# RWKV trunk: one substitution for the triangular inverses of two batches

## The chip, the cores and the metric

One core of a Trainium2 chip runs one program. TensorE (PE) multiplies, VectorE (DVE), ScalarE (ACT) and GpSimd (POOL) work element by element, SyncE (SP) issues most DMAs. The metric is the device time of one execution in microseconds. The shapes are one sequence of 512 tokens with 1024 features, all in float32.

## The reference

The model has two layers. Layer 0 mixes tokens with RWKV-7, layer 1 with a spatial gating unit; each is followed by a SwiGLU feed-forward network, and each of the four parts has a norm ahead of it and one behind it. The change touches the RWKV-7 mixer alone. Its core is a recurrence over the 512 tokens for each of 16 heads of 64 features:

```python
def step(S, inp):
    r_t, w_t, k_t, v_t, a_t, b_t = inp
    sa = jnp.einsum('bhij,bhj->bhi', S, a_t)
    S = (S * w_t[:, :, None, :]
         + sa[..., None] * b_t[:, :, None, :]
         + v_t[..., None] * k_t[:, :, None, :])
    y = jnp.einsum('bhij,bhj->bhi', S, r_t)
    return S, y
```

k, r and v are projections of differently mixed inputs; w (the decay) and a come from small two-layer projections; after the recurrence come a group norm per head, a bonus term, a gate and the output projection.

## The kernel before, in words

The kernel does the recurrence by chunks of 64 tokens, 8 chunks per head. Inside a chunk the terms with a and b form a lower triangular matrix of 64 x 64 whose inverse (of identity minus it) is needed once per head and chunk. The 1024 features are taken in four batches b of 256 features, which is 4 heads, so 32 matrices of 64 x 64 a batch. A matrix is cut in four blocks of 32: the two on the diagonal are inverted, and the block below is put together from them by products.

The work is written in stages, each for one batch: P (projections of k and r), E (`early`: decay, its cumulated sums, the scaled copies that go to the scratch tensors sa and sb in HBM), F (`front`), B (`back`), S (`scan`, the state from chunk to chunk), N (group norm, gate). X makes the mixed input for v, split in a high and a low part for three-pass products, and V multiplies it with the weights of v for one batch. X holds eight tiles `xsp` of 128 features; the string XV says in which pool of SBUF each of them lives: x (the pool of the input tiles), s and e (pools whose slots other tiles of the same size use too).

`front` loads ST and MV from scratch, multiplies them (`lm`, L709: four products for four chunks of one head), and takes three things from each result: VectorE masks a part into MV (L712), ScalarE copies the triangular part to LA (L715) and another part to BX (L716). `bkt` (L722) are transposes by products, copied by ScalarE to BX (L726, L727).

`back` inverts. VectorE transposes LA in blocks of 32 to LX (L735). POOL multiplies LA by a mask (L738), so that only the blocks of 16 below the diagonal of each block of 32 stay for the later products. Then a substitution of 15 steps runs on VectorE, with two instructions each (L744 product, L746 sum into Dm), on all 128 diagonal blocks of 16 of the batch at once (m16 is the mask's column). Dm starts as identity, which POOL writes in `front` (L696, L697). Two block transposes give Dn (L749, in the tile `hn`) and Dt (L750). From there TensorE joins blocks: Qp (L766, from LA and Dn), Qs on VectorE, Np and Tp (L775, L778), copies to Dn2 and bdT, Q2p (L789), a copy, T2p (L798), a copy to bdT (L802). `mvt` (L757) transposes MV; mp (L807) multiplies MVt with the finished inverse, ScalarE copies the result (L809), and gh (L814) multiplies on; VectorE adds the results into MV (L816, L817). `scan` takes MV (us L843, Yp L856).

What sets the order: the list PLAN gives the order in which the stages are recorded. A scheduler of the framework, which simulates the recorded program, then sets the order on each engine from the recorded order, the dependences and its own idea of times. Slots of SBUF are given out in the recorded order too: a tile waits until the last reader of the slot's former tile is done. Each engine runs its own queue strictly in order. `E3` is the last early stage; its chain ends on VectorE with `ta` (L662) and on POOL with two products (L669 with r, L670 with kp), after which `bps` (L665, the bonus term) and the stores to sb follow.

Of the kernel before, what the change touches and what calls it, by code (L numbers as in the profile page):

```python
# [32 lines left out]
PLAN = "P0 E0 P1 P2 E1 P3 E2 E3 X0 F0 B0 F1 V0 V1 V2 V3 B1 S0 F2 S1 F3 N0 B2 N1 B3 S2 N2 S3 N3".split()  # L33
XV = "xxxessss"
# [48 lines left out]
class Trunk:  # L83
# [287 lines left out]
    def rwkv(self, x0, nxt):  # L371
# [3 lines left out]
        with ExitStack() as ctx:  # L375
# [23 lines left out]
            def gslot(name, shape):  # L399
                return self.gp.tile(shape, F32, name=name, tag="gain", bufs=2)  # L400
# [21 lines left out]
            m16 = mk2[:, 0, 0:C:16]  # L422
# [184 lines left out]
            diag = lambda t: t[:, :, 0:512].rearrange("p b (t s) -> p b t s", s=32)  # L607

# [69 lines left out]
            def front(b, o):  # L678
# [13 lines left out]
                LA = e2("LA", (P, 2, NC, C))  # L692
                Dm = self.f0p.tile([P, 2, 528], F32, name="Dm", tag="f0", bufs=2)
                for hd in range(2):
                    g.memset(LA[64 * hd + 32:64 * hd + 64, :, :, 0:32], 0.0)
                g.memset(full(Dm), 0.0)  # L696
                g.memset(Dm.rearrange("p b r -> p (b r)")[:, 0:1024:33], 1.0)  # L697
                for hh, q in units:
# [6 lines left out]
                    for hd in range(2):  # L705
                        rows, other = head[hd], head[1 - hd]
                        lm = self.bank("pl", "lm")
                        for cc in range(4):
                            mm(lm[:, cc * P:(cc + 1) * P], st[:, cc].rearrange("p n t -> p (n t)"), mv[:, :, cc, hd, :], start=True, stop=True)  # L709
                        lv = lm.rearrange("p (c a t) -> p c a t", c=4, a=2)  # L710
                        la = LA[:, q, 4 * hh:4 * hh + 4]
                        v.tensor_tensor(mv[other, :, :, hd].rearrange("p a c t -> p c a t"), lv[other],  # L712
                                        mk2[other].unsqueeze(1).broadcast_to([64, 4, 2, C]), op=ALU.mult)
                        for z, x in ((64 * hd, 0), (64 * hd + 32, 32)):
                            a.copy(la[z:z + 32, :, x:C], lv[z:z + 32, :, 0, x:C])  # L715
                        a.copy(bx[rows, 1], lv[rows, :, 1, :])  # L716
# [11 lines left out]
                o.update(MV=MV, BX=BX, LA=LA, Dm=Dm)  # L728

            def back(b, o):  # L730

                MV, BX, LA, Dm = (o[n] for n in ("MV", "BX", "LA", "Dm"))
                LX = e2("LX", (P, 2, 528))

                v.transpose(full(LX), LA.rearrange("p q c (x t) -> p t (q c x)", x=2))  # L735
                LAu = LA.rearrange("p q c t -> p (q c) t")
                LAs = LA.rearrange("p q c (x t) -> p (q c) x t", t=16)
                g.tensor_tensor(LAs, LAs, m16.unsqueeze(1).unsqueeze(3).broadcast_to([P, 16, 4, 16]), op=ALU.mult)  # L738
# [8 lines left out]
                Dt = rp.tile([P, 16, 2, 32], F32, name="Dt", tag="hid", bufs=1)  # L747
                Dn = self.sm.tile([P, 16, 2, 32], F32, name="hn", tag="hn", bufs=2)
                v.transpose(Dn.rearrange("p u x s -> p s (u x)"), full(Dm).rearrange("p t s -> p s t"))  # L749
                v.transpose(Dt.rearrange("p u x t -> p t (u x)"), full(Dm))  # L750
# [13 lines left out]
                for u in range(16):  # L764
                    for z, hd, x in quarters:
                        mm(Qp[z:z + 32, u * 32:(u + 1) * 32], LAu[z:z + 32, u, 32 * x:32 * x + 32], Dn[z:z + 32, u, x, :],  # L766
                           start=True, stop=True)
# [4 lines left out]
                for u in range(16):  # L772
                    for z, hd, x in quarters:
                        if x == 0:
                            mm(Np[z:z + 32, u * 32:(u + 1) * 32], Dt[z:z + 32, u, x, :], Qs[z:z + 32, u, :], start=True, stop=True)  # L775
                for u in range(16):
                    for z, hd, x in quarters:
                        mm(Tp[z:z + 32, u * 32:(u + 1) * 32], Qs[z:z + 32, u, :], Dt[z:z + 32, u, x, :], start=True, stop=True)  # L778
# [8 lines left out]
                for u in range(16):  # L787
                    for z in (0, 64):
                        mm(Q2p[z + 32:z + 64, u * 32:(u + 1) * 32], LAu[z:z + 32, u, 32:64], Dn2[z:z + 32, u, :],  # L789
                           start=True, stop=True)  # L790
# [159 lines left out]
            for n in PLAN:  # L950
# [188 lines left out]
```

## Time and profile before

| | |
|---|---|
| median of 3 runs | 1424.42 us (1421.11 to 1426.13) |
| the profiled execution | 1426.41 us, span 1424.7 us |
| busy TensorE, VectorE, ScalarE, POOL | 1338.3, 791.8, 569.1, 274.5 us |
| share of TensorE in the chain that ended last | 77% (VectorE 7%) |

A row of the grouped view gives the line, the engine, the operation, output and inputs by the program's names, the count, then busy time in us and mean ns of one, then the idle time of the engine ahead of them and what ended it. A row of a time line gives start and length in us; the bracket behind it is idle time of that engine and what released it. A row of the waits reads: who <- for whom: us in total, times, longest. The table of stretches has for each engine busy time and count of instructions, then the granted clock of TensorE as a share of the full one, the share of busy DMA and GB/s. The profile counts most products twice: where the order has 4 `lm`, the trace has 8.

### The profile page before, as it was taken

How to read it: one execution, taken by the hardware profiler on the slowest of the kernel's cores; microseconds unless marked ns; L12 is line 12 of the kernel's file. 1: busy time of each engine (PE TensorE's matmuls, PEld its weight loads, DVE VectorE, ACT ScalarE, POOL GpSimd, SP SyncE). 2: the span in 40 equal slices, each digit the busy share in tenths (PEclk: the TensorE clock that was granted, in tenths of full speed). 3: DMA queues.
4: the chain of work that ended last, by engine and by line, in shares of the span. 5: the costliest groups of instructions: out<-in, count | busy, mean ns of one | idle time of the engine just before them, and what ended most of it. 6: DMA issues, size and time to landing. Idle time of an engine off the chain costs nothing.

```text
span 1424.7 us, 21481 instructions
## 1 busy us (share of the span) xinstructions
PE 1338.3 (94%) x8472; PEld 1091.2 (77%) x8472; DVE 791.8 (56%) x1318; ACT 569.1 (40%) x1060; POOL 274.5 (19%) x248
## 2 busy tenths in 40 slices
PE   5899997987889979999999999999999999999998
PEld 3576686976768768888888888778888888888886
DVE  6962776388685775554544222865575455443223
ACT  5654665363723363323322122743363232322221
POOL 6154463133311231111111000210121111110000
PEclk9999998987969989999999999999999999999999
DMA  5133467351322423333332232343213333332331
GB/s 157 30 107 92 127 182 200 94 150 43 87 65 88 130 90 104 89 89 103 90 99 94 89 118 74 104 129 109 89 52 112 103 89 89 103 90 103 89 96 67
DMA packets 210324, 143.04 MB, mean 100 GB/s; under 512 B 59664, under 2 KB 185136, under 8 KB 210224
## 3 DMA queue, kind: packets, MB, share of 16 engines
q1 hardware_dynamic: 208544, 135.90, 32.2%
q0 software_dynamic: 1680, 5.77, 1.3%
q8 instruction: 67, 1.10, 0.3%
q14 instruction: 33, 0.27, 0.1%
HBM read 125.39 MB, written 14.16 MB: 98 GB/s over the span
## 4 chain that ended last, share of the span: by engine, by line
PE 77%; DVE 7%; ACT 2%; issue 2%; DMA 2%; POOL 1%; SPq 1%; DVEq 0%; POOLq 0%; ACTq 0%
PE gu L158 12%; PE gu L156 12%; PE gu L157 12%; PE acc L156 8%; PE acc L157 8%; PE acc L158 8%; PE gh L814 2%; PE lm L709 2%; PE u L156 1%; PE u L158 1%; PE u L157 1%; PE Yp L856 1%; PE mp L807 1%; PE proj L158 1%; PE proj L156 1%
## 5 line engine op out<-in xcount | busy, mean ns | idle before, releaser
L131 ACT CAST whi<-wraw 128x1024 fp32r<-128x1024 f32 x161 | 168.8, 1050 | 472.5 <-PE gu L157 257.2
L132 DVE TENSOR_TENSOR wlo<-wraw,whi 128x1024 fp32r<-128x1024 f32 x161 | 246.6, 1532 | 197.2 <-ACT whi L131 193.2
L157 PE MATMUL gu<-hT,whi 128*128 128x512 f32 (+1 forms) x768 | 289.6, 378 | 4.4 <-DVE hT L59 4.4
L156 PE MATMUL gu<-hT,whi 128*128 128x512 f32 (+1 forms) x768 | 290.2, 380 | 0.8 <-ACT hT L57 0.8
L158 PE MATMUL gu<-hT,wlo 128*128 128x512 f32 (+1 forms) x768 | 289.7, 378 | 0.0
L157 PEld LDWEIGHTS gu<-hT,whi 128*128 128x128 f32 x768 | 146.0, 190 | 34.0 <-DVE hT L59 4.7
L156 PEld LDWEIGHTS gu<-hT,whi 128*128 128x128 f32 x768 | 145.8, 191 | 29.5 <-ACT hT L57 1.0
L158 PEld LDWEIGHTS gu<-hT,wlo 128*128 128x128 f32 x768 | 145.8, 190 | 29.0 <-issue 0.2
L157 PE MATMUL acc<-wlo,act 128*128 128x512 f32 x416 | 163.9, 394 | 0.0
L156 PE MATMUL acc<-whi,act 128*128 128x512 f32 x416 | 163.6, 394 | 0.0
L158 PE MATMUL acc<-whi,act 128*128 128x512 f32 x416 | 160.5, 394 | 0.0
L333 POOL TENSOR_TENSOR sg<-sg,hn 128x512 f32<-128x512 f32 x44 | 56.7, 1288 | 422.5 <-DVE sg L332 422.5
L332 DVE TENSOR_TENSOR sg<-sg,gu 128x512 f32<-128x512 f32 x44 | 30.2, 687 | 142.5 <-PE gu L158 141.1
L148 POOL TENSOR_TENSOR wlo<-wraw,whi 128x1024 fp32r<-128x1024 f32 x28 | 70.1, 2505 | 169.9 <-ACT whi L147 151.1
L158 PEld LDWEIGHTS acc<-whi,act 128*128 128x128 f32 x416 | 78.2, 188 | 18.1
L156 PEld LDWEIGHTS acc<-whi,act 128*128 128x128 f32 x416 | 78.2, 188 | 18.0
L157 PEld LDWEIGHTS acc<-wlo,act 128*128 128x128 f32 x416 | 78.1, 188 | 18.0
L330 DVE TENSOR_TENSOR sg<-gu,hn 128x512 f32<-128x512 f32 x44 | 30.4, 691 | 67.8 <-PE gu L158 67.6
L131 ACT CAST act<-sg 128x512 fp32r<-128x512 f32 x52 | 32.3, 622 | 72.2 <-POOL sg L333 58.1
L158 PE MATMUL proj<-xsp,wlo 128*128 128x512 f32 x128 | 53.7, 421 | 0.0
L156 PE MATMUL proj<-xsp,whi 128*128 128x512 f32 x128 | 51.9, 405 | 0.4 <-ACT k L529 0.4
L709 PE MATMUL lm<-MV,ST 128*128 128x128 f32 x256 | 41.6, 316 | 11.2 <-DMA ST<-sb 7.9
(305 smaller groups left out, 2248.8 us busy)
## 6 DMA issues: line engine op xcount, KB each, us to landing
wraw<-in_ffn_w_gate_dram SPq DMA_DIRECT2D x44, 512.0 KB, 3.6
wraw<-in_ffn_w_up_dram SPq DMA_DIRECT2D x44, 512.0 KB
wraw<-in_ffn_w_down_dram SPq DMA_DIRECT2D x44, 512.0 KB, 3.6
wraw<-in_rwkv_w_rkv_dram SPq DMA_DIRECT2D x24, 512.0 KB, 3.5
wraw<-in_sgu_w_in_dram SPq DMA_DIRECT2D x16, 512.0 KB, 3.6
x<-in_x_dram SPq DMA_DIRECT2D x8, 512.0 KB, 3.7
MV<-sa SPq DMA_DIRECT2D x64, 64.0 KB, 2.6
ST<-sb SPq DMA_DIRECT2D x8, 512.0 KB, 4.5
```

Source lines behind the costliest of these rows:

```text
L131: self.nc.scalar.copy(hi, src)
L132: self.nc.vector.tensor_tensor(lo, src, hi.bitcast(F32), op=ALU.subtract)
L148: nc.gpsimd.tensor_tensor(lo, raw, hi.bitcast(F32), op=ALU.subtract)
L156: mm(out, lhs[0], rhs[0], start=start, stop=False)
L157: mm(out, lhs[0], rhs[1], start=False, stop=False)
L158: mm(out, lhs[1], rhs[0], start=False, stop=stop)
L330: nc.vector.tensor_tensor(sg, pp[0], yb, op=ALU.mult)
L332: nc.vector.tensor_tensor(sg, sg, pp[1], op=ALU.mult)
L333: nc.gpsimd.tensor_tensor(sg, sg, yb, op=ALU.mult)
L709: mm(lm[:, cc * P:(cc + 1) * P], st[:, cc].rearrange("p n t -> p (n t)"), mv[:, :, cc, hd, :], start=True, stop=True)
L807: mm(mp[:, cc * P:(cc + 1) * P], bdT[:, q * NC + 4 * hh + cc].rearrange("p h t -> p (h t)"), mt[:, cc, :], start=True, stop=True)
L814: mm(gh[:, cc * P:(cc + 1) * P], mt[rows, cc, :], bx[rows, 0:2, cc, :], start=True, stop=True)
```

## The change

Batches 0 and 1, and batches 2 and 3, share one substitution. There is a new stage I (`inverses`, n = 0 or 1), recorded after the fronts of both batches. LA is now a tile of (P, 2, 2, 8, 32) for both batches with the diagonal blocks of 32 alone, a second tile LB of the same size holds the blocks below the diagonal, and one transpose, one substitution and two transposes back do for all 256 diagonal blocks of 16 of a pair. Before, half of LX and Dm held blocks off the diagonal, whose result no product read. `front` fills LA and LB with three copies of 32 x 128 for each head's `lm` (L719, L720, L721) where there were two copies, one of them of double width; the memset of LA's empty blocks is gone, and Dm is written once for a pair. POOL's mask product is replaced by a ScalarE activation with a scale per partition (f16, L744) and a memset on POOL (L745). Dn moves from the pool of `hn` to the e slots.

PLAN is changed too: V0 to V3 stand after F0 and ahead of F1, and I0, B0, B1 follow F1; I1 stands after F3. XV becomes "xxxxeegs": tiles 4 and 5 of the input for v live in e slots, tile 6 in a slot of the pool "gain", which holds two tiles and in E3 is that of the cumulated sums, tile 7 in s.

```diff
-PLAN = "P0 E0 P1 P2 E1 P3 E2 E3 X0 F0 B0 F1 V0 V1 V2 V3 B1 S0 F2 S1 F3 N0 B2 N1 B3 S2 N2 S3 N3".split()
-XV = "xxxessss"
+PLAN = "P0 E0 P1 P2 E1 P3 E2 E3 X0 F0 V0 V1 V2 V3 F1 I0 B0 B1 S0 F2 S1 F3 I1 N0 B2 N1 B3 S2 N2 S3 N3".split()
+XV = "xxxxeegs"
...
-            m16 = mk2[:, 0, 0:C:16]
+            f16 = rp.tile([P, 1], F32, name="f16")
+            for r in range(0, P, 32):
+                a.copy(f16[r:r + 32], mk2[r:r + 32, 0, (16 if r % 64 == 0 else 48):][:, 0:1])
...
-                    new = dict(x=xslot, s=s4, e=e2)[where[kt]]
+                    new = dict(x=xslot, s=s4, e=e2, g=gslot)[where[kt]]
...
-                LA = e2("LA", (P, 2, NC, C))
-                Dm = self.f0p.tile([P, 2, 528], F32, name="Dm", tag="f0", bufs=2)
-                for hd in range(2):
-                    g.memset(LA[64 * hd + 32:64 * hd + 64, :, :, 0:32], 0.0)
-                g.memset(full(Dm), 0.0)
-                g.memset(Dm.rearrange("p b r -> p (b r)")[:, 0:1024:33], 1.0)
+                if b % 2 == 0:
+                    LA, LB = (e2(n, (P, 2, 2, NC, 32)) for n in ("LA", "LB"))
+                    Dm = self.f0p.tile([P, 2, 528], F32, name="Dm", tag="f0", bufs=2)
+                    g.memset(full(Dm), 0.0)
+                    g.memset(Dm.rearrange("p b r -> p (b r)")[:, 0:1024:33], 1.0)
+                    lower[b // 2] = LA, LB, Dm
+                LA, LB, _ = lower[b // 2]
...
-                        for z, x in ((64 * hd, 0), (64 * hd + 32, 32)):
-                            a.copy(la[z:z + 32, :, x:C], lv[z:z + 32, :, 0, x:C])
+                        z = 64 * hd
+                        a.copy(la[z:z + 32], lv[z:z + 32, :, 0, 0:32])
+                        a.copy(lb[z:z + 32], lv[z:z + 32, :, 0, 32:64])
+                        a.copy(la[z + 32:z + 64], lv[z + 32:z + 64, :, 0, 32:64])
...
+            def inverses(n):
+                LA, LB, Dm = lower.pop(n)
                 LX = e2("LX", (P, 2, 528))
-                v.transpose(full(LX), LA.rearrange("p q c (x t) -> p t (q c x)", x=2))
-                LAu = LA.rearrange("p q c t -> p (q c) t")
-                LAs = LA.rearrange("p q c (x t) -> p (q c) x t", t=16)
-                g.tensor_tensor(LAs, LAs, m16.unsqueeze(1).unsqueeze(3).broadcast_to([P, 16, 4, 16]), op=ALU.mult)
+                LAu, LBu = (t.rearrange("p b q c t -> p (b q c) t") for t in (LA, LB))
+                v.transpose(full(LX), LAu.rearrange("p u t -> p t u"))
+                a.activation(LAu[:, :, 16:32], LAu[:, :, 16:32], AF.Copy, scale=f16[:, 0:1])
+                g.memset(LAu[:, :, 0:16], 0.0)
...
-                Dn = self.sm.tile([P, 16, 2, 32], F32, name="hn", tag="hn", bufs=2)
+                Dn = e2("Dn", (P, 32, 32))
...
+                return LAu, LBu, Dn, Dt
+
+            def back(b, o, inv):
+                MV, BX = o["MV"], o["BX"]
+                LAu, LBu, Dn, Dt = (t[:, b % 2 * 16:b % 2 * 16 + 16] for t in inv)
...
+                elif f == "I":
+                    inv = inverses(b)
                 elif f == "B":
-                    back(b, ops[b])
+                    back(b, ops[b], inv)
```

Line numbers move: in the changed kernel L709 is L713, L722 is L728, L735 is L742, L744 and L746 are L751 and L753, L749 and L750 are L756 and L757, L757 is L770, L766 is L779, L802 is L814, L807 is L819, L814 is L826; in `early`, L669 and L670 are L672 and L673.

The scheduler makes the order on the engines from this. Three places follow. First TensorE just after the two `ssp` (sums of squares) of E3; the number behind a name is that of the tile. Before:

```order
L709 MATMUL lm_1526<-MV_1478,ST_1476 128x128 x4
L647 MATMUL ssp_1389<-tw_1349,bones_135 128x512
L156 MATMUL v_2317<-whi_2321,xsp_1431 128x256
L157 MATMUL v_2317<-wlo_2322,xsp_1431 128x256
L158 MATMUL v_2317<-whi_2321,xsp_1431 128x256
```

The change:

```order
L650 MATMUL ssp_1390<-tw_1354,bones_135 128x512
L650 MATMUL ssp_1394<-tw_1354,bones_135 128x512
L713 MATMUL lm_1521<-MV_1483,ST_1481 128x128 x4
L713 MATMUL lm_1531<-MV_1483,ST_1481 128x128 x4
L668 MATMUL bps_1404<-hsel_141,ta_1355 64x2 x16
L728 MATMUL bkt_1542<-ident_79,ST_1481 128x128 x4
L713 MATMUL lm_1554<-MV_1490,ST_1481 128x128 x4
L156 MATMUL v_1650<-whi_1708,xsp_1472 128x256
L157 MATMUL v_1650<-wlo_1709,xsp_1472 128x256
```

Before, products of v with tiles that were ready followed at once, and `bps` stood far behind; now `bps` and the first `bkt` are ahead of them, and the next product of v reads xsp_1472, which is tile 6. On ScalarE its cast stands here in the change:

```order
L653 ACTIVATE tw_1354<-tw_1354 128x1024
L719 COPY LA_1513<-lm_1521 32x128
L719 COPY LA_1513<-lm_1531 32x128
L720 COPY LB_1514<-lm_1521 32x128
L721 COPY LA_1513<-lm_1521 32x128
L722 COPY BX_1518<-lm_1521 64x256
L720 COPY LB_1514<-lm_1531 32x128
L721 COPY LA_1513<-lm_1531 32x128
L722 COPY BX_1518<-lm_1531 64x256
L131 CAST xsp_1472<-xs_1469 128x512
```

Before, all tiles of the input for v were cast ahead of the L653's equivalent; now one is cast after the first copies of the front. LA_1513 takes the slot of E3's r, LB_1514 that of E3's k, and xsp_1472 that of E3's cumulated sums. The second place is TensorE ahead of the first Qp. Before:

```order
L156 MATMUL v<-whi,xsp 128x256
L157 MATMUL v<-wlo,xsp 128x256
L158 MATMUL v<-whi,xsp 128x256
L766 MATMUL Qp<-hn,LA 32x32 x64
```

The change:

```order
L713 MATMUL lm<-MV,ST 128x128 x12
L728 MATMUL bkt<-ident,ST 128x128 x4
L713 MATMUL lm<-MV,ST 128x128 x4
L728 MATMUL bkt<-ident,ST 128x128 x4
L770 MATMUL mvt<-ident,MV 128x128 x24
L779 MATMUL Qp<-Dn,LA 32x32 x64
L787 MATMUL Np<-Qs,Dt 32x32 x32
L790 MATMUL Tp<-Dt,Qs 32x32 x64
```

Between the last `lm` of F1 and the first Qp there are now 4 `bkt` and 24 `mvt`, and no product of v is left behind it; before, products of v stood on both sides of each of these groups. The third place is TensorE ahead of the third Qp, that of batch 2, in the change:

```order
L713 MATMUL lm<-MV,ST 128x128 x4
L868 MATMUL Yp<-su,MV 64x64 x3
L728 MATMUL bkt<-ident,ST 128x128 x4
L770 MATMUL mvt<-ident,MV 128x128 x24
L939 MATMUL yt<-ident,Y 128x128 x4
L779 MATMUL Qp<-Dn,LA 32x32 x64
L156 MATMUL gate<-sg,g2h 128x512
```

Before, the third Qp came in pieces between the `lm` of F3 (24, 3, 1, 11, 10, 3, 6 and 6 of 64); now it stands behind the last of them.

More of the change, by code (lines that the diff above doesn't have):

```diff
@@ L397, in xslot, with gslot @@
                 return self.xp.tile(shape, dt, name=name, tag="x", bufs=TT)
-            def gslot(name, shape):
-                return self.gp.tile(shape, F32, name=name, tag="gain", bufs=2)
+            def gslot(name, shape, dt=F32):
+                return self.gp.tile(shape, dt, name=name, tag="gain", bufs=2)
             mk2 = rp.tile([P, 2, C], F32, name="mk2")
@@ L607, in rwkv @@
             diag = lambda t: t[:, :, 0:512].rearrange("p b (t s) -> p b t s", s=32)
+            lower = {}
             def early(b, k, r):
@@ L746, in back @@
                     v.tensor_tensor(Dmd[:, :, j + 1:16, 0:j + 1], Dmd[:, :, j + 1:16, 0:j + 1], tv, op=ALU.add)
-                Dt = rp.tile([P, 16, 2, 32], F32, name="Dt", tag="hid", bufs=1)
-                Dn = self.sm.tile([P, 16, 2, 32], F32, name="hn", tag="hn", bufs=2)
-                v.transpose(Dn.rearrange("p u x s -> p s (u x)"), full(Dm).rearrange("p t s -> p s t"))
-                v.transpose(Dt.rearrange("p u x t -> p t (u x)"), full(Dm))
+                Dt = rp.tile([P, 32, 32], F32, name="Dt", tag="hid", bufs=1)
+                Dn = e2("Dn", (P, 32, 32))
+                v.transpose(Dn.rearrange("p u s -> p s u"), full(Dm).rearrange("p t s -> p s t"))
+                v.transpose(Dt.rearrange("p u t -> p t u"), full(Dm))
+                return LAu, LBu, Dn, Dt
+            def back(b, o, inv):
+                MV, BX = o["MV"], o["BX"]
+                LAu, LBu, Dn, Dt = (t[:, b % 2 * 16:b % 2 * 16 + 16] for t in inv)
                 MVt = {}
@@ L765, in back @@
                     for z, hd, x in quarters:
[L766 to L767 removed]
+                        mm(Qp[z:z + 32, u * 32:(u + 1) * 32], LAu[z:z + 32, u, :], Dn[z:z + 32, u, :], start=True, stop=True)
                 Qs = el("Qs", (P, 16, 32))
@@ L788, in back @@
                     for z in (0, 64):
-                        mm(Q2p[z + 32:z + 64, u * 32:(u + 1) * 32], LAu[z:z + 32, u, 32:64], Dn2[z:z + 32, u, :],
+                        mm(Q2p[z + 32:z + 64, u * 32:(u + 1) * 32], LBu[z:z + 32, u, :], Dn2[z:z + 32, u, :],
                            start=True, stop=True)
```

10 lines of the change are left out of this document (4 added, 6 removed).

## The prediction

> **What bounds the kernel now.** I read the page's busy table first, then the stretches of 25 us with the granted clock, then TensorE's waits, then the time lines around the inverses.
>
> ```profile
> PE 1338.3 (94%) x8472; PEld 1091.2 (77%) x8472; DVE 791.8 (56%) x1318; ACT 569.1 (40%) x1060; POOL 274.5 (19%) x248
> ```
> ```profile
> core 0: us, PE busy (x) PEld busy (x) DVE busy (x) ACT busy (x) POOL busy (x), PEclk, DMA share, GB/s
> 188.00:425.00 237.00, 197.13 (x2696) 174.16 (x2698) 163.69 (x315) 118.86 (x286) 76.34 (x89) 0.85 0.41 114
> 550.00:880.00 330.00, 330.00 (x1421) 266.73 (x1420) 137.92 (x133) 91.06 (x110) 30.66 (x24) 1.00 0.32 97
> ```
> 94% would say that TensorE's work is all that counts, and after 550 us it is: not a gap in 330 us, clock 1.00. The change lies in 188 to 425 us, and there TensorE stands for 237.0 - 197.1 = 39.9 us and has a mean clock of 0.85. This stage is a chain across engines; what is to be read is what TensorE waits for, and what covers each wait.
>
> ```profile
> PE mp L807 <- DVE bdT L802: 12.5, 2, 7.3
> PE lm L709 <- DMA ST<-sb: 7.9, 2, 4.6
> PE Qp L766 <- issue: 4.0, 1, 4.0
> ```
> ```profile
> 391.60:396.90 5.30, 0.00 (x0) 0.00 (x0) 5.27 (x14) 0.00 (x0) 1.80 (x1) 0.50 0.14 51
> 396.90:415.50 18.60, 17.22 (x78) 14.54 (x78) 17.95 (x40) 5.45 (x10) 3.46 (x3) 0.50 0.21 71
> 415.50:418.00 2.50, 2.50 (x19) 1.99 (x18) 0.57 (x2) 0.34 (x1) 0.00 (x0) 1.00 0.15 52
> ```
> The largest wait is for T2p's copies (L802), and VectorE is full beside it (5.27 of 5.30 us): the substitution of the next batch stands in its queue. After it TensorE works for 18.6 us at half clock, 17.2 of them busy. These waits are what the change can give back.
>
> **What is removed.** The substitution is fixed work per instruction, so two of four vanish:
>
> ```profile
> L744 DVE TENSOR_TENSOR tm<-LX,Dm 128x30 f32<-128x30 f32 (+7 forms) x60 | 22.3, 372 | 1.2
> L746 DVE TENSOR_TENSOR Dm<-Dm,tm 128x30 f32<-128x30 f32 (+7 forms) x60 | 21.0, 350 | 1.3
> L749 DVE STREAM_TRANSPOSE hn<-Dm 128x1024 f32<-128x1024 f32 x4 | 8.5, 2126 | 0.1
> L750 DVE STREAM_TRANSPOSE Dt<-Dm 128x1024 f32<-128x1024 f32 x4 | 7.9, 1976 | 0.0
> L735 DVE STREAM_TRANSPOSE LX<-LA 128x1024 f32<-128x1024 f32 x4 | 7.8, 1952 | 0.8 <-ACT LA L715 0.8
> L738 POOL TENSOR_TENSOR LA<-LA,mk 128x1024 f32<-128x1024 f32 x4 | 10.8, 2712 | 3.3 <-DVE nr_y L174 2.0 <-DVE mu L878 1.2
> L715 ACT COPY LA<-lm 32x256 f32<-32x256 f32 x32 | 11.6, 361 | 29.6 <-DVE MV L712 29.2
> L715 ACT COPY LA<-lm 32x128 f32<-32x128 f32 x32 | 8.2, 257 | 0.4
> ```
> VectorE loses half of 22.3 + 21.0 + 8.5 + 7.9 + 7.8 = 67.5, that is 33.7 us. POOL loses L738, 10.8 us, and half the memsets of Dm. ScalarE gets 96 copies of the shorter form (0.257, 24.7 us) for 11.6 + 8.2 = 19.8: +5 us over four fronts, and two mask operations of about 0.5. Nobody waits for these sums as such. B1 and B3 now find their inverse ready; I give the change the whole 12.5 us at L802 for that, and take the price of the new places next.
>
> **V0 meets the end of E3.** The order shows it: after the two `ssp` TensorE has 12 `lm`, `bps` and 4 `bkt`, then products on xsp_1472. That is tile 6 of XV, which now sits in a "gain" slot that was E3's `cum`. Its cast stands on ScalarE behind eight copies into LA, LB and BX; those of LA take the slot of E3's `r`, those of LB that of E3's `k`. So it waits for POOL's L669 and L670. In the trace before these end late, and it costs nothing, as v covers it:
>
> ```profile
> 198.74 1.41 DVE L712 TENSOR_TENSOR MV<-lm,mk 64x512 f32<-64x512 f32 x2
> 200.07 2.25 DVE L132 TENSOR_TENSOR wlo<-wraw,whi 128x1024 fp32r<-128x1024 f32 x1
> 206.49 1.42 DVE L653 SCALAR_TENSOR_TENSOR k<-k,nkk,tw 128x512 f32<-128x512 f32 x2 [3.57 <-ACT tw L650]
> 212.92 1.95 DVE L662 SCALAR_TENSOR_TENSOR ta<-r,vecT,kp 128x512 f32<-128x512 f32 x2
> 215.27 2.19 POOL L669 TENSOR_TENSOR r<-r,Pp 128x1024 f32<-128x1024 f32 x1
> 217.41 2.36 POOL L670 TENSOR_TENSOR kp<-kp,cum 128x1024 f32<-128x1024 f32 x1
> ```
> ```profile
> 195.52 0.68 PE L709 MATMUL lm<-MV,ST 128*128 128x128 f32 x4 [3.23 <-DMA ST<-sb]
> 199.22 0.28 PE L157 MATMUL v<-wlo,xsp 128*128 128x256 f32 x1
> 199.34 0.28 PE L158 MATMUL v<-whi,xsp 128*128 128x256 f32 x1
> ```
> Products of v come every 0.12 us there, about 118 of them (14 us) between 199 and 220. In the new order neither the split of wlo (2.25 us, ahead of the second `tw`) nor the L712 of the later `lm` (three, 0.7 each) stand between E3's operations, and `tw` waits less for ScalarE; I let `ta` end at 209.5, not 214.9; L669 ends at 211.9 (2.19), L670 at 214.2 (2.36), the cast at about 215. TensorE can do 12 `lm`, `bps` and `bkt`, about 3 us, between 199 and 215.5: **13 us more idle**. Bounds: nothing, if E3 ran so far ahead that the cast is done by 202; and 19 us, if L670 ends at 219.8 as now. I stand nearer the upper end, since the chain from `k` to L670 alone is 206.49 to 219.77 = 13.3 us and cannot begin before ssp.
>
> **I0 has no cover.** The batches' order was B0 after F0, with V and F1 to fill. Now LX needs F1's last `lm`, and the order has all of V before it; between the last `lm` and Qp stand only 4 `bkt` and 24 `mvt`. From 215.5 the work is 312 products of v at 0.12 = 37.4, and by the rows
>
> ```profile
> 213.34 1.05 PE L709 MATMUL lm<-MV,ST 128*128 128x128 f32 x8
> 202.57 0.60 PE L722 MATMUL bkt<-ident,ST 128*128 128x128 f32 x4
> ```
> (the profile counts an `lm` twice, so 4 of the order are 8 here) 52 `lm` 14 and 28 `bkt` 4.2, and I add 7 for gates, weights and another wait for ST like the one of 4.6: last `lm` at 278. Then the copies to LA and LB (1), LX 1.95, thirty operations, and Dn:
>
> ```profile
> L744 DVE TENSOR_TENSOR tm<-LX,Dm x60: 173/270/2345, 224.8 to 408.4; 128x30 f32<-128x30 f32 x8, 128x56 f32<-128x56 f32 x8, 128x78 f32<-128x78 f32 x8, 128x96 f32<-128x96 f32 x8
> 245.34 2.21 DVE L749 STREAM_TRANSPOSE hn<-Dm 128x1024 f32<-128x1024 f32 x1
> 334.00 2.35 DVE L744 TENSOR_TENSOR tm<-LX,Dm 128x110 f32<-128x110 f32 x1
> 333.87 2.34 POOL L900 TENSOR_TENSOR Y<-Y,gn 128x1024 f32<-128x1024 f32 x1 [3.65 <-DVE Y L885]
> ```
> An operation takes 0.27 us in the median (the second number of the first row), thirty with small gaps 9 us; the 20 us from the first at 224.8 to Dn at 245.34 hold much else. Qp0 starts at 278 + 1 + 2 + 9 + 2.2 = 292, not 249.4; `mvt` (at the price of `bkt`, 24 x 0.15) takes 3.6 us of it, so **11 us are idle**. Bounds: 8 (if copies and gaps cost nothing) and 22 (as long as batch 0 takes now).
>
> **B0, B1, S0, F2, S1, F3.** Before, 132 products of v (16 us) lay between Qp0 and Qp1; now none, and B0's chain (Qp, Qs, Np and Tp, a copy, Q2p, a copy, T2p, a copy, then mp and gh) stands bare, some 5 us of it idle.
>
> ```profile
> 249.36 1.29 PE L766 MATMUL Qp<-hn,LA 32*32 32x32 f32 x128
> 265.42 0.83 PE L807 MATMUL mp<-MVt,bdT 128*128 128x128 f32 x6
> 293.75 1.71 PE L814 MATMUL gh<-BX,MVt 64*128 64x128 f32 x16
> ```
> Qp to mp was 16.1 us with 61 products of v between (7.3): bare 9. mp to the end of the last gh was 30.0 us with 71 of them (8.5) and 12 `lm` of F1: bare 20. Qp1 stands at 321. From there to F3's last `lm` TensorE has 64 `lm` (17), 32 `bkt` (5), 32 gh and 16 mp (11), the scans (9), B1's chain (5), gates and waits: 56 us, to 378.
>
> **I1 has no cover either**, and N1's group norm stands between its operations. In the order Qp2 is behind 24 `mvt` and 4 `yt`. Of the pure 15 us (LX to Dn, as at I0), the norm's five wide operations and small ones add 6.4 (about 1.2 us each, as L885 below); beside POOL's norm a VectorE operation took 2.35 us in place of 0.27, and two such add 4: 25.5 us, Qp2 at 404. **About 19 us are idle.** The chain's bounds are 15 (no norm, no POOL) and 32, what batch 3 took (from LX at 380.2 to Dn's end):
>
> ```profile
> 380.16 1.95 DVE L735 STREAM_TRANSPOSE LX<-LA 128x1024 f32<-128x1024 f32 x1
> 398.44 1.22 DVE L885 TENSOR_TENSOR Y<-Y,nr_y 128x1024 f32<-128x1024 f32 x1
> 410.55 2.06 DVE L749 STREAM_TRANSPOSE hn<-Dm 128x1024 f32<-128x1024 f32 x1
> 424.86 0.77 PE L766 MATMUL Qp<-hn,LA 32*32 32x32 f32 x67
> ```
> Then Qs is behind Dt, `ob` and a split of weights, mp2 at 417; mp2 to Qp3 took from 396.9, where TensorE's wait of 5.30 ends, to 424.86 = 28 us before, 18 of them at half clock, which doubled some 9 us of work. I take 23: **Qp3 at 440**, not 424.9. From Qp3 on both orders are alike.
>
> **Sum.** The profiled execution took 1426.41 us (span 1424.7), 2 us above the runs' median of 1424.42. 440 - 425 = +15: **1441 us**. A ledger beside it: +13 + 11 + 19 of new idle time and 5 at B0, 48; less 12.5 at L802, 4.6 at F1's ST (V0 to V3 are ahead of it now), 4 at Qp and 9 of half clock, 30: +18. I keep the walk's 15.
>
> Half clock is the term I am least sure of. The rows show it from 391.6 to 415.5 although TensorE was hardly idle from 396.9 on. The Trainium skill, TensorE: Matmul & The Clock Gate, Part 1 (The HAM clock gate), has the array at half rate after one idle window of about 3.4 us, and back after about 3.4 us of sustained work; the 18 us here contradict the second half. By that rule each of three new stretches costs 1.7 us of lag, 5 in all, and the sum would be 1446. By the row it is up to 9 each; the 23 us above hold 4 of it for one stretch.
>
> **The rivals.**
> *Faster, 1413 (0.20).* VectorE's queue is the mechanism. If E3's chain, freed of 5 us of VectorE work, ends so early that the cast is there by 205 (3 us idle, not 13), and I1 takes 18 us as L738 and half the substitution are gone, Qp3 is 440 - 10 - 7.5 = 422; with the half clock of 391 to 415 gone too (9), 413: 12 us saved. For it: 163.7 us of VectorE in the stage become 130, and 76.3 of POOL some 64. Against: the waits at xsp_1472 and LX are of dependence, not load. It decides from 20 us less than my three idle terms of 43 and the half clock.
> *No change, about 1426 (0.14).* The three idle terms at two thirds (29 of 43 us) take 14 off the walk: Qp3 at 426.
> *Worse, 1459 (0.16).* The walk has no half clock after the new idle stretches at E3 and I0; with 9 us after each, as after 396.9, Qp3 is at 458. For it: those 18 us at 0.50 follow a gap shorter than either. Against: between 550 and 880the clock is whole throughout, and I cannot see in the trace what ends a slow stretch.
>
> **How the numbers follow.** My forecast of 1441, with its own range of 1430 to 1450, has 0.50. A measurement of this kernel tells some 0.3%, 4 us, from no change. Below 1420 lies the faster rival (0.20), within 4 us of 1424 the second with an edge of my own case (0.14), the rest is slower: 0.66. The range has to leave out no more than 0.2: from 1418, which takes a part of the faster case, to 1460, the worse case's middle.
>
> **What would show it.** Right: TensorE idle before the first product on xsp_1472, its cast released by POOL's L673; idle of some 10 us ahead of the first Qp and over 15 ahead of the third, both put down to the transposes into Dn; no wait at T2p's copies; VectorE near 758 us busy. Wrong: no gap at 200 to 215, or Qp2's wait under 10 us, or TensorE's idle time in the stage below 40 us. If F2 and F3 run longer than 60 us between Qp1 and LX, ScalarE's copies set the pace, and the worse case holds for another reason than clock.

## The result and the profile after

| | before | after |
|---|---|---|
| median of the runs | 1424.03 us (1421.11 to 1426.13, 4 runs) | 1468.8 us (1455.06 to 1478.82, 4 runs) |
| ratio | 1 | 1.0281, 95% interval 1.0226 to 1.0335 |
| profiled execution | 1426.41 us, span 1424.7 | 1468.59 us, span 1466.9 |
| mean granted clock | 0.962 | 0.937 |

The changed kernel is slower by 45 us by the medians and by 40 by the ratio; 1441 had been predicted. One of its four runs, 1478.82, was in a slower state and is not in the ratio; the other three took 1455.06, 1468.59 and 1469.01 us. So every difference to this kernel is uncertain by some 8 us, and the profiled execution is not its fastest. The busy table of the page after:

```profile
PE 1351.8 (92%) x8472; PEld 1102.8 (75%) x8472; DVE 761.7 (52%) x1252; ACT 573.3 (39%) x1098; POOL 255.5 (17%) x234
```

VectorE did lose 30.1 us (791.8 to 761.7) and POOL 19. But the span grew by 42.2 us, of which 13.5 are TensorE's own busy time (1351.8 - 1338.3) with the same 8472 products, and the other 28.7 are idle time. Stretches show where: up to the fourth Qp; B0's chain and its dense part; the wait at I1; from the third group of mp, and from the fourth Qp, to the first product of the feed-forward network (`gu`). After:

```profile
core 0: us, PE busy (x) PEld busy (x) DVE busy (x) ACT busy (x) POOL busy (x), PEclk, DMA share, GB/s
188.00:452.90 264.90, 199.67 (x2688) 178.00 (x2688) 133.01 (x252) 122.90 (x324) 52.86 (x69) 0.79 0.35 98
285.60:327.10 41.50, 36.12 (x616) 32.20 (x616) 11.70 (x25) 9.42 (x21) 3.11 (x6) 0.54 0.09 21
302.00:323.70 21.70, 21.20 (x113) 18.30 (x113) 5.01 (x14) 4.03 (x10) 3.11 (x6) 0.50 0.13 29
390.40:413.20 22.80, 5.98 (x28) 4.29 (x28) 22.16 (x51) 5.88 (x11) 9.26 (x8) 0.62 0.22 65
435.10:557.30 122.20, 110.00 (x1125) 89.87 (x1123) 68.90 (x171) 46.73 (x111) 19.47 (x19) 0.88 0.26 81
452.90:557.30 104.40, 94.27 (x974) 75.97 (x972) 60.81 (x151) 39.20 (x95) 19.47 (x19) 0.86 0.28 88
```

The same view of the kernel before: from 188 to its fourth Qp, from its third group of mp to its first `gu`, and from the fourth Qp to `gu`:

```profile
188.00:424.90 236.90, 197.03 (x2684) 174.06 (x2685) 163.65 (x314) 118.86 (x286) 76.34 (x89) 0.85 0.41 114
397.00:514.70 117.70, 110.63 (x1140) 90.55 (x1140) 83.54 (x202) 47.74 (x114) 24.88 (x22) 0.91 0.31 95
424.90:514.70 89.80, 84.05 (x989) 68.35 (x988) 61.03 (x152) 39.07 (x96) 21.42 (x19) 0.98 0.34 105
```

Up to the fourth Qp the change costs 28.0 us: idle time 65.2 in place of 39.9 (+25.4), busy +2.6. From there to `gu` it costs 14.6 more: idle 10.1 for 5.8 (+4.4), busy +10.2. Behind `gu` nothing differs (909.6 and 910.0 us). What TensorE waited for between 188 and 500 us:

```profile
PE yt L939 <- DVE Y L913: 14.4, 1, 14.4
PE Qp L779 <- DVE Dn L756: 10.0, 2, 8.4
PE bps L668 <- DVE ta L665: 6.8, 1, 6.8
PE T2p L810 <- ACT bdT L795: 6.6, 2, 5.3
...
PE mp L819 <- DVE bdT L814: 1.4, 1, 1.4
```

The wait at T2p's copies, 12.5 us before, is 1.4 here. In its place stand the wait for the first inverse (8.4 at Qp), and one of 14.4 that is named after `yt`, the transposes of N1's result. These four products stand ahead of the third Qp in TensorE's queue. VectorE's time line in that wait:

```profile
390.41 1.96 DVE L742 STREAM_TRANSPOSE LX<-LA 128x1024 f32<-128x1024 f32 x1
...
392.40 0.20 DVE L751 TENSOR_TENSOR tm<-LX,Dm 128x30 f32<-128x30 f32 x1
392.52 1.22 DVE L891 TENSOR_TENSOR Y<-Y,mu 128x1024 f32<-128x1024 f32 x1
...
395.07 1.22 DVE L895 TENSOR_REDUCE va<-hn 128x16 f32<-128x1024 f32 x1 [0.16 <-ACT hn L893]
...
399.55 2.31 DVE L174 SCALAR_TENSOR_TENSOR nr_y<-nr_t,nr_y 128x16 f32<-128x16 f32 x1
...
403.92 1.22 DVE L897 TENSOR_TENSOR Y<-Y,nr_y 128x1024 f32<-128x1024 f32 x1
...
405.36 2.37 DVE L751 TENSOR_TENSOR tm<-LX,Dm 128x110 f32<-128x110 f32 x1
...
409.35 1.22 DVE L913 TENSOR_TENSOR Y<-Y,hn 128x1024 f32<-128x1024 f32 x1
...
411.18 1.98 DVE L756 STREAM_TRANSPOSE Dn<-Dm 128x1024 f32<-128x1024 f32 x1
```

The substitution and the group norm take turns, operation by operation, for 22.8 us from LX to Dn's end; `yt` starts at 410.62, when the norm's last operation there ends, and Qp at 413.30, when Dn does. Whichever of the two the row names, it is this one queue.

### The profile page after: what moved, and what is told of

It reads as the page before. It is cut to its first block, busy times and chain, and to the rows that moved or that the text cites. A ratio compares the mean times of both kernels' runs of the same rounds, so it can differ in the third digit from the quotient of the medians.

```text
span 1466.9 us, 21418 instructions
## 1 busy us (share of the span) xinstructions
PE 1351.8 (92%) x8472; PEld 1102.8 (75%) x8472; DVE 761.7 (52%) x1252; ACT 573.3 (39%) x1098; POOL 255.5 (17%) x234
## 4 chain that ended last, share of the span: by engine, by line
PE 77%; DVE 8%; ACT 3%; issue 2%; DMA 1%; POOL 1%; SPq 0%; DVEq 0%; ACTq 0%; POOLq 0%
PE gu L157 11%; PE gu L158 11%; PE gu L156 11%; PE acc L156 8%; PE acc L157 8%; PE acc L158 8%; PE lm L713 2%; PE gh L826 1%; PE Yp L868 1%; PE u L158 1%; PE u L157 1%; PE u L156 1%; PE v L156 1%; PE v L157 1%; PE mp L819 1%
## 5 line engine op out<-in xcount | busy, mean ns | idle before, releaser
L132 DVE TENSOR_TENSOR wlo<-wraw,whi 128x1024 fp32r<-128x1024 f32 x161 | 243.2, 1510 | 211.8 <-ACT whi L131 207.7
L156 PE MATMUL gu<-hT,whi 128*128 128x512 f32 (+1 forms) x768 | 289.4, 379 | 0.2 <-ACT hT L57 0.2
L156 PE MATMUL proj<-xsp,whi 128*128 128x512 f32 x128 | 51.6, 403 | 0.4 <-ACT k L531 0.4
L157 PE MATMUL proj<-xsp,whi 128*128 128x512 f32 x128 | 50.4, 397 | 0.0
```

The lines of the kernel that those rows point to most:

```text
L132: self.nc.vector.tensor_tensor(lo, src, hi.bitcast(F32), op=ALU.subtract)
L156: mm(out, lhs[0], rhs[0], start=start, stop=False)
L157: mm(out, lhs[0], rhs[1], start=False, stop=False)
```

## The experiments

Every ratio is to the kernel before, timed on the same chip.

**E3's wait: only XV put back.**

```diff
-XV = "xxxxeegs"
+XV = "xxxessss"
```

> The changed kernel with the string XV of before ("xxxessss": tile 6 of v's input not in a gain slot). The order then has 96 products of v ahead of bps, and I0 and I1 uncovered as before. If V0's wait for the end of E3 costs what the changed kernel's trace shows there (13 us idle and some 5 more through half clock between 189 and 215 us), this runs 13 to 18 us faster than the changed kernel, at 1451 to 1456 us. If the time is lost only at the two inverses and behind them, the earlier products just wait longer at I0, and it stays within 4 us of the changed kernel's 1469 us.

Measured: 1465.54 us, ratio 1.0296 (1.0263 to 1.0329): nothing gained. TensorE's waits from 188 to 300 us:

```profile
PE lm L713 <- ACT BX L733: 7.2, 3, 4.1
PE Qp L779 <- DVE Dn L756: 6.8, 1, 6.8
PE v L156 <- ACT whi L131: 3.7, 1, 3.7
PE lm L713 <- DMA ST<-sb: 3.2, 1, 3.2
```

The wait at `bps` is gone, as products of v stand ahead of it again. But the last four tiles of the input now lie in s slots, which F1's MV needs too, and F1's `lm` wait instead (7.2 us, put down to copies into BX; that the slots cause it is argued); the first Qp starts at 289.4, not 285.7. So the run has a confound: it shows that the gap at E3 is not lost on net, not that V0's slots cost nothing.

**The order without the shared substitution:** the kernel before with the new XV and new order, each batch with its own inverse.

```diff
-PLAN = "... E3 X0 F0 B0 F1 V0 V1 V2 V3 B1 S0 F2 S1 F3 N0 B2 N1 B3 ..."
+PLAN = "... E3 X0 F0 V0 V1 V2 V3 F1 B0 B1 S0 F2 S1 F3 N0 B2 N1 B3 ..."
-XV = "xxxessss"
+XV = "xxxxeegs"
```

> The kernel before, each batch with its own substitution, but with V0 to V3 ahead of F1 and XV as in the change: all of the new order, nothing of the merging. If the loss is the loss of v as cover, it has most of the 45 us: 20 us or more over before, 1444 to 1465 us. If the loss is the merged inverse, ready late and waited for by both batches, this is within 15 us of before, at most 1439 us.

Measured: 1430.56 us (10 runs), ratio 1.0043 (1.0021 to 1.0064). Its waits have the same gap at E3 as the changed kernel:

```profile
PE bps L665 <- DVE ta L662: 7.8, 1, 7.8
```

Order and slots together, this gap in them, cost 6 us. The shared substitution, with the copies and the mask that come with it, adds the other 38 (34 by the ratios).

**The substitution's latency.** The changed kernel with one of the 15 steps (the rest of the inverse is left out):

```diff
-                for j in range(15):
+                for j in range(1):
```

> The changed kernel with one of the 15 steps of the substitution left (the inverse is then not computed; the transposes into and out of it stay). 28 operations, about 8 us, leave each of the two inverses. If the latency of the two inverses sets the time at I0 and I1, it gains those 16 us and with the group norm's stalls and half clock behind them 20 to 35: 1434 to 1449 us. If other waits (E3's end, copies, the clock) take their place, it gains under 10 us: above 1459.

Measured: 1441.77 us, ratio 1.0119 (1.01 to 1.0139). 27 of the 45 us (23 of 40 by the ratios) go with these 56 instructions, 16.2 us of VectorE's time (761.7 - 745.5). The page:

```profile
PE 1339.0 (93%) x8472; PEld 1093.0 (76%) x8472; DVE 745.5 (52%) x1196; ACT 573.8 (40%) x1098; POOL 256.7 (18%) x234
```

The span fell by 26.9 us, and 12.8 of them are TensorE's busy time, which is back at that of before (1339.0 and 1338.3). That the wait had lowered the clock does not follow from this; the run with both cuts, below, speaks against it for B0's chain.

**The same cut in the kernel before** (again one of 15 steps).

> The kernel before with one of the 15 steps left in each of the four substitutions (the inverses are not computed). The same cut gave the changed kernel 27 us for two substitutions. If the substitution is covered in the kernel before, it gains less than 10 us here, 1415 or more. If it is VectorE's load that counts, four substitutions gain about twice as much as two: 1375 to 1390. If both count alike, by latency of those not covered (batches 1 and 3), 15 to 27 us: 1397 to 1409.

Measured: 1420.94 us, ratio 0.9975 (0.9958 to 0.9991): 3.6 us. The kernel before does four substitutions, and without nearly all of their steps it gains 3.6 us; the change halves these steps and so had less than that to win from them. (The transposes around them and POOL's mask, of which the change saves a part too, stay in this run.) In the changed kernel the two substitutions that are left are worth 27. The wait at T2p's copies fell from 12.8 to 5.6 us (188 to 500 us), but others grew (5.0 at `us` for MV, 4.5 at T2p for a copy of ScalarE): over the whole run TensorE's idle time rose from 86.4 to 91.4 us, and its busy time fell by 11.1. So the busy time falls with the steps by nearly as much here, where no inverse is shared, as in the changed kernel (12.8).

**The two pairs apart.** One pair keeps the shared substitution, the other goes back to one for each batch, in the changed kernel's order.

```diff
+MERGED = (0,)      # or (1,)
...
-                if b % 2 == 0:
+                if b // 2 not in MERGED:
...
+                elif b % 2 == 0:
```

> The changed kernel (its PLAN and XV) with batches 2 and 3 not merged: I1 is gone, they have a substitution each as before. Between the unmerged order (1430.6) and the changed kernel (1469) stand 38 us. If both merges cost alike, by their latency, this stands in the middle, 1445 to 1455 us. If I1 is the dear one (14.4 us of idle time in one piece and half clock to 437 us), this gains 25 us or more: 1435 to 1445.

> The changed order with batches 0 and 1 not merged: I0 is gone, I1 stays. If both merges cost alike: 1445 to 1455 us. If I1 is the dear one: 1455 to 1465. The two halves should add: e6 and e7 over 1430.6 should sum to about 38 us if the merges act each by itself, to much less if one hides the other.

Measured: batches 0 and 1 alone 1453.07 us, ratio 1.0196 (1.0164 to 1.0227); 2 and 3 alone 1446.91 us, ratio 1.0170 (1.0138 to 1.0202). Over the order's 1430.56 that is 22 and 16 us by the medians, together 39, where both at once add 38 (22, 18 and 34 by the ratios). Each pair costs on its own; neither alone is the culprit.

**Batches 2 and 3 shared in the order of before** (old PLAN and XV, but I1 behind F3).

```diff
-PLAN = "... S0 F2 S1 F3 N0 B2 N1 B3 ..."
+PLAN = "... S0 F2 S1 F3 I1 N0 B2 N1 B3 ..."
```

> The kernel before (its PLAN and XV) with batches 2 and 3 merged alone: products of v still cover B0 and B1. VectorE loses one substitution, POOL one mask. If a merge pays where nothing else is moved, this is below before: 1410 to 1420 us. If the uncovered latency of I1 decides, it costs what e7 costs over the unmerged order: 1436 to 1450.

Measured: 1439.4 us (6 runs), ratio 1.0104 (1.0072 to 1.0137), some 15 us. The loss does not hang on the new place of V.

**N1's norm.** The changed kernel without batch 1's group norm (left out of the computation):

```diff
-                    group_norm(b, o, Y, tts)
+                    if b != 1:
+                        group_norm(b, o, Y, tts)
```

> The changed kernel without batch 1's group norm (left out entirely: its 5 wide and about 15 small VectorE operations, the POOL and ScalarE ones). It stood between the operations of I1's substitution. If sharing VectorE with the norm costs I1 the 10 us that I gave it, this gains 10 to 14 us: 1455 to 1459. If I1 waits for the chain of the substitution's own operations, 5 us or less.

Measured: 1455.28 us, ratio 1.0214 (1.0187 to 1.0242): 13.5 us less (some 10 by the ratios).

**Both cuts at once:** without batch 1's norm and with one step.

> The changed kernel with 1 of the 15 steps of each substitution and without batch 1's group norm (both left out of the computation). The loss is 45 us; cutting the substitution alone gave 27, leaving the norm out alone 13.5. Theory A, two separate additions to the same chain (the substitution's operations stand one behind the other on VectorE, and the norm's stand between them or ahead of the products on Y): the gains add, 1468.8 - 27 - 13.5 = 1428, within 4. Theory B, the norm costs only because it stretches the substitution, so with the substitution gone there is little left to take: 1438, at most 4 us below the 1441.8 of the run without substitution. In theory A what is left over the kernel before is the price of the order and the projections' slots alone, some 6 us; in B 14 us have still another cause.

Measured: 1426.09 us (10 runs), ratio 1.0025 (0.9999 to 1.0051). 1468.8 - 1426.1 = 42.7, and 27 + 13.5 = 40.5: the two add (theory A). The step from the run without substitution to this one, 1441.8 to 1426.1, needs no time of the changed kernel and its spread: it is 15.7 us (13 by the ratios), where theory B allowed 4. But only the sum is that of theory A. The same stretches of TensorE's queue in the four traces, one execution each, in us:

| | changed | one step | no norm of batch 1 | both cuts |
|---|---|---|---|---|
| start to first Qp | 285.7 | 280.1 | 288.1 | 278.7 |
| first to second Qp (B0) | 41.5 | 37.1 | 41.5 | 41.9 |
| second to third Qp | 86.2 | 66.1 | 78.9 | 66.8 |
| third to fourth Qp | 39.6 | 42.0 | 36.7 | 39.5 |
| fourth Qp to `gu` | 104.4 | 105.3 | 98.2 | 91.9 |

The substitution costs at the two waits: 5.6 us ahead of the first Qp and 20.0 ahead of the third. The norm costs 7.3 us ahead of the third Qp where it shares VectorE with the substitution, and nothing there where the substitution is gone (66.1 and 66.8). Then it costs 13.5 behind the fourth Qp. The stretch from the fourth Qp to `gu`, with one step and with both cuts:

```profile
425.32:530.66 105.34, 91.78 (x973) 74.28 (x973) 61.98 (x152) 38.98 (x95) 19.47 (x19) 0.90 0.29 88
426.87:518.72 91.85, 83.51 (x974) 66.88 (x972) 60.93 (x151) 39.08 (x95) 19.68 (x19) 1.00 0.34 101
```

With the norm in, 5.2 us more are idle there and the clock is lower; why the norm of batch 1 acts so late was not tried. And B0's chain takes 41.9 us with both cuts, at a clock of 0.59, although TensorE waits just 0.8 us for Dn ahead of it:

```profile
278.68 1.28 PE L779 MATMUL Qp<-Dn,LA 32*32 32x32 f32 x128 [0.80 <-DVE Dn L756]
278.68:320.59 41.91, 35.42 (x620) 31.19 (x620) 11.61 (x25) 9.46 (x21) 3.11 (x6) 0.59 0.09 21
```

So the half clock in B0's chain does not hang on the wait ahead of it. (It varies: with one step the chain took 37.1 us at 0.72, behind as short a wait.) On the whole, TensorE's busy time in this run is 1336.3 us, that of before 1338.3. With both cuts nearly nothing of the loss is left, so the rest of the change, which this run has too (the third copy for each head, the mask on ScalarE, Dn in e slots), can cost little unless the cuts hide it. What the norm costs in the kernel before was not tried. If that kernel pays for its norm too, as it pays 3.6 us for the substitution, as much of the loss is not explained by these cuts.

**Wide products in the waits.** The changed kernel with products of 512 columns, which nothing reads, put in both waits for the inverse, to hold the clock:

```diff
+                wide = self.bank("pt", "wide")
+                for k in range((8, 14)[n]):
+                    mm(wide, self.ident, LX.rearrange("p b r -> p (b r)")[:, 512 * (k % 2):512 * (k % 2) + 512],
+                       start=True, stop=True)
```

> The changed kernel with idle time filled: 8 and 14 products of the identity with 512 columns of LX, whose result nobody reads, stand on TensorE while the two merged inverses are computed. They add work but no dependence that the substitution has to wait for. If half clock after the two waits is what the 13.5 us of longer busy time are (1351.8 against 1338.3), the clock stays at 1.00 through B0 (285 to 324 us, now 0.5) and the time falls by 8 to 14 us, to 1455 to 1461. If the narrow products of B0 and B2 hold the clock low by themselves, it stays within 4 us of 1469 or loses the fill's own time.

Measured: 1468.25 us, ratio 1.029 (1.0249 to 1.0331): no change. Stretches of it in the first wait and behind it:

```profile
277.00:288.60 11.60, 9.07 (x32) 4.50 (x31) 10.54 (x33) 2.20 (x4) 0.53 (x1) 1.00 0.00 1
290.00:300.00 10.00, 6.47 (x305) 6.06 (x295) 3.00 (x5) 2.88 (x5) 0.00 (x0) 0.50 0.02 5
300.00:310.00 10.00, 7.88 (x84) 7.11 (x79) 2.20 (x5) 1.16 (x2) 0.63 (x2) 0.50 0.01 2
310.00:320.00 10.00, 9.95 (x53) 8.24 (x52) 1.79 (x5) 2.75 (x6) 1.44 (x3) 0.52 0.23 52
```

The clock stays whole through the filled wait, and is at 0.50 right behind it, in B0's small products. The long wait alone is not what lowers it.

**Wide products in B0's and B2's chains as well** (2 ahead of Np, 6 around Q2p).

```diff
...
+                wide = self.bank("pt", "wide")
+                for k in range(3 * (b % 2 == 0)):
+                    mm(wide, self.ident, Qs.rearrange("p u s -> p (u s)"), start=True, stop=True)
...
```

> As the filled kernel (8 and 14 wide products in the two waits), with 8 more wide products set between the small ones of B0 and of B2 (2 ahead of Np, 6 around Q2p), where TensorE has gaps of 0.8 to 1.5 us. In the filled kernel the clock was 1.00 until the first Qp and 0.50 from 290 us. If gaps between the small products lower the clock, it now stays up through B0 and the time falls by 8 us or more, to about 1460 or below. If the small and narrow products lower it whatever stands between them, the clock still falls to 0.5 within 5 us of the first Qp and the time is 1467 or more.

Measured: 1477.36 us, ratio 1.0378 (1.0344 to 1.0412).

```profile
290.00:295.00 5.00, 4.84 (x199) 3.23 (x198) 0.97 (x2) 1.73 (x3) 0.00 (x0) 0.97 0.02 3
295.00:300.00 5.00, 5.00 (x74) 2.51 (x72) 0.40 (x1) 0.58 (x1) 0.00 (x0) 1.00 0.01 3
305.00:310.00 5.00, 4.27 (x23) 3.75 (x22) 0.78 (x3) 0.58 (x1) 0.00 (x0) 0.50 0.00 0
310.00:320.00 10.00, 9.95 (x51) 8.40 (x52) 2.52 (x7) 2.75 (x6) 2.07 (x4) 0.50 0.20 46
```

TensorE's time line has the first mp behind a short wait:

```profile
304.04 2.08 PE L831 MATMUL mp<-MVt,bdT 128*128 128x128 f32 x8 [1.39 <-DVE bdT L826]
```

With the chain filled the clock stays near 1.00 to 300 us, and falls all the same when mp and gh begin; it stays at 0.50 to 320 although TensorE is busy for 9.95 of 10 us. The run is 9 us slower than the filled one by the medians (12 by the ratios): the added products cost more than they save.

**POOL's mask alone on ScalarE.** One part of the change in the kernel before: L738's product as four activations.

```diff
-                g.tensor_tensor(LAs, LAs, m16.unsqueeze(1).unsqueeze(3).broadcast_to([P, 16, 4, 16]), op=ALU.mult)
+                for k in range(4):
+                    a.activation(LAs[:, :, k, :], LAs[:, :, k, :], AF.Copy, scale=m16[:, k:k + 1])
```

> The kernel before with the mask product of POOL (L738) done by four ScalarE activations with a scale per partition, nothing else changed. One part of the change alone: the VectorE operations that took 1.9 to 2.4 us beside it fall to 0.3. If these stalls lie on the path, it gains 3 to 8 us: 1416 to 1421. If VectorE has slack where they fall, it is within 4 us of before.

Measured: 1436.72 us, ratio 1.0101 (1.0037 to 1.0166). Neither expectation held: it is slower by 11 us by the medians, with a wide interval. The wait at T2p's copies is still 10.7 us, and behind it the clock is low for longer, to 428 us in place of 415.5:

```profile
393.00:428.00 35.00, 27.25 (x166) 22.86 (x163) 27.98 (x62) 7.78 (x15) 6.79 (x5) 0.50 0.18 55
```

TensorE's busy time rose by 7.6 us. That the four activations, in ScalarE's queue ahead of copies that TensorE waits for, set this off is argued, not shown. The changed kernel has one such activation for a pair, and has it in the run with both cuts too, where nearly nothing of the loss is left.

## Why the prediction failed

The direction was right, the size a third of what came. By its own steps:

**E3 (13 us of idle time at xsp_1472).** The size was near, 10.0 us of waits; the place and what held TensorE were not those named. Products of v resume at 211.57 (walk: 215.5), and the first of them waits for nothing that the profile shows. POOL's L673 ends at 209.2 and the cast follows at 209.8, as said, but TensorE stands ahead of that: 6.8 us at `bps` for VectorE's `ta`, and 3.2 at the first `bkt` for ScalarE's copies. These stood behind copies into LA, which waited 9.1 us for E3's r (POOL's L672). The rows of the three engines:

```profile
203.84 1.88 PE L668 MATMUL bps<-hsel,ta 128*64 128x2 f32 x32 [6.78 <-DVE ta L665]
...
206.87 2.34 POOL L673 TENSOR_TENSOR kp<-kp,cum 128x1024 f32<-128x1024 f32 x1
206.95 0.52 ACT L719 COPY LA<-lm 32x128 f32<-32x128 f32 x2 [9.12 <-POOL r L672]
...
209.80 0.62 ACT L131 CAST xsp<-xs 128x512 fp32r<-128x512 f32 x1
...
211.57 0.56 PE L156 MATMUL v<-whi,xsp 128*128 128x256 f32 x1
```

The walk counted 118 products of v between 199 and 220 in the kernel before; the trace has 96 there. F1's last `lm` is done at 270.3 (walk: 278). The slots and the order are worth 6 us on net, as the unmerged kernel shows.

**I0 (11 us idle, Qp0 at 292).** Qp0 started at 285.7 and the row gives 8.4 of idle time; with F1's last `lm` 8 us earlier than walked, the chain was 1.4 us longer. Right.

**I1 (25.5 us from LX to Dn, 19 idle, Qp2 at 404).** LX to Dn's end took 22.8, TensorE was idle for 16.8 of them (5.98 busy in 22.80 us), and Qp2 came 25 us behind the last `lm` (walk: 26). It stands at 413.3 only because what lies before it was late. Right. For the norm 10.4 us had been booked: LX to Dn's end takes 12.7 us at I0, where no norm is near, and 15.1 at I1 in the run without the norm, so the norm's part is 8 to 10 us. The 13.5 us of that run are not all of this place, as the table above shows.

**The half clock: the step that failed.** "Less [...] 9 of half clock" was booked as a gain, since the 18.6 us at 0.50 behind T2p's copies would go with the wait. B0's chain was walked at 29 us, from pieces that had run mostly at full clock between products of v. It took 41.5 us, with just 5.4 idle (5 booked) and the rest at a clock of 0.54. These are rows from the dense part of it, against 0.83 for six mp and 1.71 for 16 gh in the prediction:

```profile
302.45 3.09 PE L826 MATMUL gh<-BX,MVt 64*128 64x128 f32 x16 [0.73 <-ACT MVt L821]
305.88 2.08 PE L819 MATMUL mp<-MVt,bdT 128*128 128x128 f32 x8
```

Sixteen gh took 1.8 times as long. From Qp2 to mp2 it was 21.8 us for 13 walked: half clock, and 5.3 us of T2p's wait for ScalarE, which stood 4.9 us ahead of a cast that a DMA released, with the copies for T2p behind it. In the ledger's terms: its idle terms alone give 48 - 12.5 - 4.6 - 4 = +27, and idle time rose by 25.4 up to the fourth Qp and 4.4 behind it. (That this fits is in part luck: the three large terms came to 10.0 + 8.4 + 16.8 = 35 us for 43, and T2p's wait, which the sum does not have, made up for some of it.) Half clock was to give back 9; busy time rose by 2.6 up to the fourth Qp, and by 10.2 behind it. The term was mis-sized by 9 + 2.6 + 10.2 = 22 of the 24 us that the ledger missed (42.2 - 18); the walk, with its +15, missed 27.

**"From Qp3 on both orders are alike."** In products yes, in time no: Qp3 to `gu` took 104.4 us for 89.8. Only 4.4 of it is idle time (its largest new waits are 2.5 at gh for N's `nr_y` and 1.9 at the gate for `ob`); the rest is half clock, from 464 to 477 and from 491 to 501. Counted from the third group of mp the busy time is the same (110.0 and 110.6 us). So as much half clock as had stood between mp2 and Qp3, and was booked as given back, stood a little later, behind Qp3; what B0's and B2's chains lost ahead of mp2 was new. Qp3 is 13 us behind the walk, and 14.6 more were lost behind it.

**The rivals.** The worse case (1459: half clock behind each new idle stretch, 9 us each) came nearest by its time; it had 0.16. It named the cost that was missing, but not what brings it: B0's chain is at half clock with the wait ahead of it filled (0.50 from 290 us) and with that wait cut to 0.8 us (0.59). And it was priced for two stretches at most, and half clock came at four places: behind E3, in B0's chain, at I1 and in B2's, and behind Qp3. The faster case (VectorE's load as the mechanism) falls with the cut in the kernel before: the steps of the substitution were worth 3.6 us. The case of no change needed the three large idle terms at 29 of 43 us; they came to 35, and half clock came with them.

**The rule weighed in the prediction.** The Trainium skill, TensorE: Matmul & The Clock Gate, Part 1 (The HAM clock gate), has the full clock back after some 3.4 us of sustained work. Here it was not back within the 21.7 us from 302 to 323.7, 21.2 of them busy. By that rule the prediction's estimate was 1446; the longer row was the nearer one.

The cause in short: sharing the substitution saves work that other work covered (its steps were worth 3.6 us in the kernel before), and makes each inverse wait for two fronts, so that it starts when little is left to cover it. Its latency, with N1's norm between its operations at I1, is then paid. This the cuts show: 5.6 and 20.0 us at the two waits. The rest of the loss is half clock, where the prediction had a gain. It is shown as a cost, by the 13.5 us more of TensorE's busy time; what brings it stays open. In B0's chain it is there without the long wait, and behind Qp3 it goes with batch 1's norm (0.90 with it, 1.00 without it, where the substitution is cut).

## What to carry to other kernels

Ask of work that is to be saved what covers it now: cut it away in a throw-away version, and what the time drops by (3.6 us here) bounds what saving it can give there. A merge of two pieces of work makes both wait for the later input, so price the latency of the merged piece at the point where the cover has run out, and put a neighbour that shares its engine on the same bill (with a group norm between its operations the inverse took 22.8 us, alone 12.7). Where wide products are taken out from between small ones, price the small ones at the slow clock of the trace too, not only at the duration they have between wide ones.

## What was not expected of the hardware

The granted clock stays at 0.50 through long stretches in which TensorE is all but fully busy: 21.2 of 21.7 us in the changed kernel (302 to 323.7), 9.95 of 10 in both filled versions (0.52 and 0.50). In these the products are narrow (64 to 128 columns: mp, gh, us, Yp). But width alone does not decide. Two more stretches of the changed kernel:

```profile
437.60:452.90 15.30, 13.94 (x144) 12.29 (x144) 8.08 (x21) 6.36 (x15) 0.00 (x0) 1.00 0.14 44
492.67:501.40 8.73, 8.73 (x41) 7.10 (x42) 5.20 (x13) 1.02 (x4) 3.96 (x4) 0.50 0.60 193
```

The first has the same narrow products at full clock; the second is at half clock without a gap, and holds products of 512 columns (`acc`). The clock comes back at 323.7 with no gap and no wide product in sight, among narrow ones; in the stretch of wide products that filled the first wait it never fell (1.00 for 11.6 us at 9.07 busy). So neither TensorE's busy share nor the width of the products decides alone; whether it is the count of rows or a longer memory of what ran before is open, and no version here tells these apart. Of the versions that compute everything none beat the kernel before.
